# A hybrid decoder layer in split fp32: SBUF pools in a new order, and the first down-projection steps fetched during the last up unit

## The chip, the cores and the metric

One core of a Trainium2 chip. The metric is the device time of one execution in microseconds. The kernel before takes 1019.38 us in the median of 3 runs (1019.26 to 1019.62). In this text 1 KB is 1024 bytes, and an address is an offset within one of SBUF's 128 partitions.

## The reference

One decoder layer over x of 1024 positions by 1024 channels, all in float32, with two sublayers, each followed by a residual and a layer norm:

```python
h = x @ w_in + b_in                                   # 1024 -> 2048
u, v = split(gelu(h[:, :1024]))                       # 4 heads of 128
y_a = u * (causal(w_spatial) @ layernorm(v) + b_spatial)   # in chunks of 128 positions
y_b = silu(layernorm(conv31(a * sigmoid(g))))         # causal depthwise conv, 31 taps; a, g = the rest of h
x1 = layernorm(2**0.25 * x + concat(y_a, y_b) @ w_out + b_out)
h2 = conv3(x1 @ w_up)                                 # 1024 -> 2*2816, causal depthwise conv, 3 taps
out = layernorm(2**0.25 * x1 + (silu(h2[:, :2816]) * h2[:, 2816:]) @ w_down)
```

## The kernel before

**Numbers.** Each operand of a matmul is split into two fp32r tiles: hi, a ScalarE copy (`split`, line 73), and lo, the rest (line 76, on VectorE or GpSimd). A product is three matmuls: hi·hi, hi·lo, lo·hi. A matmul here has weights of 128x128 and a moving operand of 128x512.

**Input projection** (`mm_steps`, L213). 16 tiles of w_in, two of them interleaved at first, each over 8 tiles of x by 2 halves by 3. The weights are `w..h` and `w..l`, the moving operands `xhi` and `xlo`. VectorE computes the 31-tap convolution meanwhile (L261).

**Output projection** (`out_steps`, L535). For each of 8 position tiles s, over 8 tiles k of w_out. The weights are `yah`, `yal`, `ybh`, `ybl`, the moving operands `woh` and `wol`; tile 0 of w_out lies in pool `w`. Then the layer norm, the transposes (`x1_T`, `x1_T2`) and sums (`x1_sums`) that make x1's operands for the up projection.

**Up units.** Unit 0 is plain (L771). Units 1 to 21 each make one gate tile and one value tile (PSUM `upg`, `upv`) by a Strassen-like scheme of 7 products instead of 8 (`prod`, L623), each of 4 k by 3 = 12 matmuls. The moving operands are b11, b21, b22 (pool `a`) and t1 to t4 (pool `f`), the weights are split per unit by `prep_unit`. `unit` keeps partial results in raw tiles `pa`, `pb` (last read at L720 and L719). `gate_tile` and `value_tile` do the 3-tap convolution (L632 on ScalarE, L635 on VectorE), the gate and the product (L649), and store the result to DRAM as `hd[f]` (L651). Odd units use the PSUM pool `un`, even ones `mm`.

**Down projection.** 2 halves th of the positions by 22 steps f. `down_prep(th, f)` (L809) loads w_down[f] (`dr`, SP's queue) and splits it into `dh` and `dl` (pool `a`), loads `hr` from `hd[f]` and splits it into `ho` (hi and lo). `down_mm` (L822) has `ho` as the weights and `dh`, `dl` as the moving operand; for each step 4 position tiles s by 2 halves by 3 = 24 matmuls. Steps are prepared two ahead. Tiles s = 0 and 1 of a half accumulate in the PSUM pool `dn`, which takes the place of `un`; s = 2 and 3 in `mm`. The last 4 steps of the second half are done tile by tile, with the final layer norm (`finish`) behind each.

**Order.** The program is written in the order of the steps, and a list scheduler at compile time arranges the instructions of all engines from it by priority (written order) and by a model of when things are ready. Each engine then runs its list in order. A tile waits until the earlier tile in its buffer has been read; a pool opened after others were closed takes their addresses and waits for them.

**Pools** (lines 48 to 54, and where they are opened), with their addresses in the program as built; the first 16 KB are a DMA scratch area:

| pool | holds | KB |
|---|---|---|
| const | columns, identity, ones | 16.1 to 19.0 |
| w | 3 raw tiles, 2 `whi`, 2 `wlo` of 4 KB | 19.0 to 47.0 |
| a | 16 tiles of 4 KB (tag A) | 47.0 to 111.0 |
| xr | 8 tiles of 4.1 KB | 111.0 to 144.0 |
| r | 3 tiles of 4 KB | 144.0 to 156.0 |
| st | small rows | 156.0 to 158.3 |
| b, then f, then g | 16 tiles of x and w_out; then 16 tiles t1 to t4; then 4 `hr` of 2 KB and 6 `ho` of 4 KB | 158.4 to 222.4 (g to 190.4) |

Of the kernel before, what the change touches and what calls it, by code (L numbers as in the profile page):

```python
# [43 lines left out]
def build(tc, xT, x, w_in, w_out, w_up, w_down, cvec, wsT, rows, bsp, out):  # L44
# [3 lines left out]
    with tc.tile_pool(name="const", bufs=1) as cp, tc.tile_pool(name="w", bufs=1) as wp, tc.tile_pool(  # L48
        name="a", bufs=16
    ) as ap_, tc.tile_pool(name="xr", bufs=8) as xp, tc.tile_pool(name="r", bufs=3) as rp, tc.tile_pool(  # L50
# [13 lines left out]
        def load(src, name, pool=None, tag="raw", eng=None):  # L64
# [60 lines left out]
        with tc.tile_pool(name="b", bufs=16) as bp, tc.tile_pool(name="ps", bufs=2, space=PSUM) as psp:  # L125
# [7 lines left out]
            warm = wp.tile([P, 1024], F32, tag="raw", name="warm", bufs=3)  # L133
# [7 lines left out]
            def raw_w(i):  # L141
                w_raw[i] = wp.tile([P, 1024], F32, tag="raw", name=f"wr{i}", bufs=3)
# [423 lines left out]
            def x1_T(s):  # L566
                so = s % 4
                if so == 0:
                    xb[0, 0], xb[1, 0] = xop("b11"), xop("b21")
                    braw.extend(wp.tile([P, 2, 512], F32, tag="raw", name=f"braw{i}", bufs=3) for i in range(2))  # L570
# [43 lines left out]
        with tc.tile_pool(name="f", bufs=1) as fp:  # L614
            ups, uw = {}, {}

            def unit_ps(f, pool, tag):
                ups[f] = [pool.tile([P, 1024], F32, tag=tag, name=f"up{q}{f}", bufs=2) for q in "gv"]

            def prod(out, w, x, first, last):  # L620
                for k in range(4):
                    for i, (a, b) in enumerate(((0, 0), (0, 1), (1, 0))):
                        nc.tensor.matmul(  # L623
                            out, w[a][:, ts(k, P)], x[b][k // 2][:, k % 2],
                            start=first and k == 0 and i == 0, stop=last and k == 3 and i == 2,
                            skip_group_check=True,
                        )

            def conv3(ct, ps, c, halves=((0, 1024),)):
                w = lambda k: col(C_CFW + 3 * ct + k)  # L630
                for a, b in halves:
                    nc.scalar.activation(c[:, a:b], ps[:, a:b], AF.Identity, bias=col(C_CFB + ct), scale=w(2))  # L632
                    for k, sh in ((1, 1), (0, 2)):
                        o = max(a, sh)
                        nc.vector.scalar_tensor_tensor(  # L635
                            out=c[:, o:b], in0=ps[:, o - sh : b - sh], scalar=w(k), in1=c[:, o:b], op0=ALU.mult,
                            op1=ALU.add,
                        )

            def gate_tile(f, halves=((0, 1024),)):  # L640
                cg = rp.tile([P, 1024], F32, tag="R", name=f"cg{f}")
                conv3(f, ups[f][0], cg, halves)
                nc.scalar.activation(cg, cg, AF.Silu)
                return cg

            def value_tile(f, cg, halves=((0, 1024),)):
                cval = rp.tile([P, 1024], F32, tag="R", name=f"cv{f}")
                conv3(NF + f, ups[f][1], cval, halves)
                nc.vector.tensor_tensor(out=cg, in0=cg, in1=cval, op=ALU.mult)  # L649
                hd[f] = dp.tile([P, S], F32, name=f"hd{f}")  # L650
                nc.sync.dma_start(hd[f], cg)  # L651

            raws = {}

            def xt(name):
                return xp.tile([P, PAD + S], F32, tag="x", name=name)[:, 0:1024]

            def load_unit(f):
                if f < NF:
                    raws[f] = []  # L660
                    for i in range(2):
                        t = xt(f"ur{f}_{i}")
                        nc.sync.dma_start(t, w_up[f + i * NF])
                        raws[f].append(t)

            def op_tile(name, n):
                if n % 2:
                    t = wp.tile([P, 1024], F32R, tag=("whi", "wlo")[n // 2 % 2], name=name, bufs=2)
                else:
                    t = A(F32R, name)  # L670
                return t[:, 0:512], t[:, 512:1024]

            nop = [0]

            def split_op(raw, name):
                hi, lo = op_tile(name, nop[0])
                nop[0] += 1
                split(raw, hi, lo, nc.scalar, nc.gpsimd)
                return hi, lo

            def prep_unit(f):
                if f >= NF:
                    return
                (g, v), tt = raws[f], nc.vector.tensor_tensor
                a11, a12, a21, a22 = g[:, 0:512], g[:, 512:1024], v[:, 0:512], v[:, 512:1024]
                sa, sb = xt(f"sa{f}"), xt(f"sb{f}")
                s1, s2, s3, s4 = sa[:, 0:512], sa[:, 512:1024], sb[:, 0:512], sb[:, 512:1024]
                w = uw[f] = {}
                w[1] = split_op(a11, f"wa{f}")
                w[2] = split_op(a12, f"wb{f}")  # L690
                tt(out=s1, in0=a21, in1=a22, op=ALU.add)
                tt(out=s2, in0=s1, in1=a11, op=ALU.subtract)  # L692
                w[6] = split_op(s2, f"ws2{f}")
                w[5] = split_op(s1, f"ws1{f}")
                tt(out=s3, in0=a11, in1=a21, op=ALU.subtract)  # L695
                w[7] = split_op(s3, f"ws3{f}")
                tt(out=s4, in0=a12, in1=s2, op=ALU.subtract)
                w[3] = split_op(s4, f"ws4{f}")
                w[4] = split_op(a22, f"wd{f}")

            def unit(f):
                z, y = ups[f][0][:, 0:512], ups[f][0][:, 512:1024]
                x, w22 = ups[f][1][:, 0:512], ups[f][1][:, 512:1024]
                w = uw[f]
                sa = wp.tile([P, 1024], F32, tag="raw", name=f"pa{f}", bufs=3)
                sb = wp.tile([P, 1024], F32, tag="raw", name=f"pb{f}", bufs=3)
                p1, u2, p5 = sa[:, 0:512], sa[:, 512:1024], sb[:, 0:512]
                v = nc.vector.tensor_tensor
                prod(x, w[1], xb[0, 0], True, False)
                prod(z, w[2], xb[1, 0], True, True)  # L710
                nc.scalar.copy(p1, x)  # L711
                prod(x, w[6], xt_[2], False, False)
                v(out=z, in0=z, in1=p1, op=ALU.add)
                prod(y, w[5], xt_[1], True, False)
                nc.scalar.copy(u2, x)
                prod(x, w[7], xt_[3], False, False)
                nc.scalar.copy(p5, y)
                prod(y, w[3], xb[1, 1], False, True)
                v(out=w22, in0=x, in1=p5, op=ALU.add)  # L719
                v(out=y, in0=y, in1=u2, op=ALU.add)  # L720
                prod(x, w[4], xt_[4], False, True)


            xt_ = {}
            with tc.tile_pool(name="tx", bufs=2, space=PSUM) as txp:
                xb[0, 1], xb[1, 1] = xop("b12"), xop("b22")
                for i in range(1, 5):
                    xt_[i] = xop(f"t{i}", fp)

                def x1_T2(s):  # L730
                    so, t = s % 4, xs_[s]
                    sl = ts(so, P)
                    tps = []
                    for g in range(2):
                        tp = txp.tile([P, 4, P], F32, tag=f"tx{g}", name=f"x1u{s}_{g}")
                        for c in range(4):
                            nc.tensor.transpose(tp[:, c], t[:, ts(g * 4 + c, P)], ident)
                        for i in range(2):
                            split(
# [47 lines left out]
                for q in range(2):  # L787
                    first_steps(q, 1, range(KT))
# [191 lines left out]
```

## Time and profile before

| | |
|---|---|
| median of 3 runs | 1019.38 us |
| the profiled execution | 1018.94 us |
| its span, first to last instruction | 1017.1 us |
| mean granted TensorE clock | 0.988 |
| instructions | 11752, of them 4344 matmuls |

In the rows further down, PE is TensorE, PEld its weight load, DVE VectorE, ACT ScalarE, POOL GpSimd, SP SyncE, and SPq SP's DMA queue. L822 is line 822 of the kernel. `pd<-dh,ho` means that tile pd is written from dh and ho. Times are in us from the start of the span unless they are marked ns; `x12` counts instructions. An arrow in brackets says how long the engine idled before and what ended it.

### The profile page before, as it was taken

What the parts mean: (1) busy time and instruction counts of PE and PEld (TensorE: products, weight loads), DVE (VectorE), ACT (ScalarE), POOL (GpSimd) and SP (SyncE); (2) the same over time, 40 slices, a digit from 0 to 9 for tenths busy, and PEclk for the clock granted to TensorE, in tenths of its full rate; (3) what the DMA queues carried; (4) which work ended last, traced back from release to release, by engine and by line L of the source; (5) the groups of instructions that cost most, each with busy time, mean ns of one, the idle gap of its engine ahead of it and who ended that gap; (6) DMA issues with size and microseconds to landing.
All of it is one profiled execution on the core that took longest, in us unless ns stands there. A gap on an engine that the chain in (4) does not pass through costs nothing.

```text
span 1017.1 us, 11752 instructions
## 1 busy us (share of the span) xinstructions
PE 988.5 (97%) x4344; PEld 798.4 (78%) x4344; DVE 677.2 (67%) x890; ACT 443.5 (44%) x661; POOL 532.5 (52%) x341
## 2 busy tenths in 40 slices
PE   8999999999997899999999999999979999999996
PEld 5888888878886678888888888888868888888885
DVE  4798999986489975665665675675454444672417
ACT  5233764854624644444443453453444323343302
POOL 4145944684916974454454454544436544488402
PEclk9999999999998899999999999999989999999999
DMA  8111121311520231132122123123458534336202
GB/s 318 60 42 43 42 104 42 125 63 42 187 83 21 84 125 63 63 105 81 63 87 100 63 83 104 63 75 111 153 184 294 175 126 154 132 129 234 98 0 83
DMA packets 33177, 106.84 MB, mean 105 GB/s; under 512 B 3680, under 2 KB 4064, under 8 KB 33120
## 3 DMA queue, kind: packets, MB, share of 16 engines
q1 hardware_dynamic: 33120, 106.09, 30.0%
q8 instruction: 34, 0.56, 0.2%
q14 instruction: 23, 0.19, 0.1%
HBM read 86.16 MB, written 19.92 MB: 104 GB/s over the span
## 4 chain that ended last, share of the span: by engine, by line
PE 87%; DVE 8%; DMA 2%; ACT 1%; issue 1%; SPq 0%; DVEq 0%; ACTq 0%
PE pd L822 24%; PE upv L623 21%; PE ps L213 16%; PE upg L623 16%; PE po L535 8%; DMA xraw<-in_xT 1%; DVE tq L757 1%; DVE wol L76 1%; DVE tq L756 1%; DVE sa L692 1%; PE sv L374 1%; DVE cg L635 1%; DMA hr<-hd 0%; DVE sb L695 0%; ACT woh L73 0%
## 5 line engine op out<-in xcount | busy, mean ns | idle before, releaser
L822 PE MATMUL pd<-dh,ho 128*128 128x512 f32 x688 | 216.4, 395 | 5.7 <-ACT ho L73 5.7
L822 PEld LDWEIGHTS pd<-dh,ho 128*128 128x128 f32 x688 | 129.8, 189 | 38.5 <-ACT ho L73 6.1
L76 POOL TENSOR_TENSOR dl<-dr,dh 128x1024 fp32r<-128x1024 f32 x44 | 108.6, 2476 | 97.7 <-ACT dh L73 97.7
L76 DVE TENSOR_TENSOR ho<-hr,ho 128x512 fp32r<-128x512 f32 x44 | 87.0, 1988 | 105.9 <-ACT ho L73 105.9
L822 PE MATMUL pd<-dl,ho 128*128 128x512 f32 x344 | 138.1, 401 | 0.0
L261 DVE SCALAR_TENSOR_TENSOR acc<-ybin,cv,acc 128x512 f32<-128x512 f32 x196 | 134.3, 747 | 0.9 <-ACT acc L255 0.3
L76 POOL TENSOR_TENSOR ws<-sb,ws 128x512 fp32r<-128x512 f32 x42 | 55.5, 1322 | 83.7 <-ACT ws L73 83.7
L73 ACT CAST dh<-dr 128x1024 fp32r<-128x1024 f32 x44 | 46.1, 1048 | 121.1 <-issue 80.7
L822 PEld LDWEIGHTS pd<-dl,ho 128*128 128x128 f32 x344 | 65.2, 189 | 14.9
L719 DVE TENSOR_TENSOR upv<-upv,pb 128x512 f32<-128x512 f32 x21 | 14.7, 699 | 86.2 <-PE upv L623 86.2
L76 POOL TENSOR_TENSOR ws<-sa,ws 128x512 fp32r<-128x512 f32 x42 | 58.7, 1400 | 7.8 <-ACT ws L73 7.5
L635 DVE SCALAR_TENSOR_TENSOR cg<-upg,cv,cg 128x1023 f32<-128x1023 f32 (+4 forms) x46 | 56.6, 1231 | 8.2 <-ACT cg L632 7.5
L76 POOL TENSOR_TENSOR wa<-ur,wa 128x512 fp32r<-128x512 f32 x21 | 27.5, 1311 | 63.9 <-ACT wa L73 61.5
L623 PE MATMUL upv<-t2h,ws 128*128 128x512 f32 x168 | 57.5, 404 | 1.9 <-ACT pa L711 1.9
L623 PE MATMUL upg<-b21h,wb 128*128 128x512 f32 x168 | 58.2, 391 | 0.5 <-POOL wb L76 0.5
L73 ACT CAST ws<-sb 128x512 fp32r<-128x512 f32 x42 | 26.1, 622 | 74.6 <-PE upv L623 72.2
L635 DVE SCALAR_TENSOR_TENSOR cv<-upv,cv,cv 128x1023 f32<-128x1023 f32 (+4 forms) x46 | 56.6, 1231 | 1.0 <-ACT cv L632 0.4
L623 PE MATMUL upg<-t1h,ws 128*128 128x512 f32 x168 | 56.5, 397 | 0.0
L623 PE MATMUL upv<-t4h,wd 128*128 128x512 f32 x168 | 56.4, 396 | 0.0
L623 PE MATMUL upv<-t3h,ws 128*128 128x512 f32 x168 | 56.3, 396 | 0.0
L623 PE MATMUL upv<-b11h,wa 128*128 128x512 f32 x168 | 55.5, 392 | 0.5 <-DVE cg L635 0.3
L623 PE MATMUL upg<-b22h,ws 128*128 128x512 f32 x168 | 55.3, 390 | 0.0
(411 smaller groups left out, 2354.3 us busy)
## 6 DMA issues: line engine op xcount, KB each, us to landing
ur<-in_w_up SPq DMA_DIRECT2D x44, 512.0 KB, 3.5
dr<-in_w_down SPq DMA_DIRECT2D x44, 512.0 KB, 4.0
hd<-cg SPq DMA_DIRECT2D x22, 512.0 KB, 2.9
hr<-hd SPq DMA_DIRECT2D x44, 256.0 KB, 3.2
wr<-in_w_in SPq DMA_DIRECT2D x14, 512.0 KB, 3.2
xres<-in_x SPq DMA_DIRECT2D x8, 512.0 KB, 3.5
wor<-in_w_out SPq DMA_DIRECT2D x8, 512.0 KB, 3.2
x1d<-xres SPq DMA_DIRECT2D x8, 512.0 KB, 2.6
```

The costliest lines, as they stand in the source:

```text
L73: nc.scalar.copy(hi, raw)
L76: lo_eng.tensor_tensor(out=lo, in0=raw, in1=hi.bitcast(F32), op=ALU.subtract)
L213: nc.tensor.matmul(ps[hf] if isinstance(ps, list) else ps[:, ts(hf, 512)], wt[:, ts(k, P)], xt(k, hf), start=first and k == 0, stop=(not f ...
L261: nc.vector.scalar_tensor_tensor(out=xs(0) if k == 0 else acc, in0=xs(k), scalar=w(k), in1=first if n == 0 else acc, op0=ALU.mult, op1=ALU ...
L374: nc.tensor.matmul(sv[:, c], a[:, g * 4 + c], whl[:, b, h], start=i == 0, stop=i == 2)
L535: nc.tensor.matmul(po[:, ts(hf, 512)], a, b[:, ts(hf, 512)], start=first and i == 0, stop=last and i == 2)
L623: nc.tensor.matmul(out, w[a][:, ts(k, P)], x[b][k // 2][:, k % 2], start=first and k == 0 and i == 0, stop=last and k == 3 and i == 2, ski ...
L635: nc.vector.scalar_tensor_tensor(out=c[:, o:b], in0=ps[:, o - sh : b - sh], scalar=w(k), in1=c[:, o:b], op0=ALU.mult, op1=ALU.add,)
L692: tt(out=s2, in0=s1, in1=a11, op=ALU.subtract)
L719: v(out=w22, in0=x, in1=p5, op=ALU.add)
L756: tt(out=t3[:, q], in0=t2[:, q], in1=raw, op=ALU.subtract)
L822: nc.tensor.matmul(pd, hh[f][a][:, ts(s % 4, P)], wd[f][b][:, c0:c1], start=first and i == 0, stop=last and i == 2,)
```

## The change

The line numbers are those of the kernel before; a piece that was only moved to another indentation is left out.

1. Pools `w`, `a`, `b` now stand one after the other behind `const`. Pool `b` stays open to the end: it holds x and w_out, then t1 to t4 (before in `f`), then `ho` (before in `g`), all in tag B with 16 buffers. Raw tiles have a pool of their own, `raw`, with 3 buffers of 4 KB and 3 for `hr` (before 4). Pools `f` and `g` are gone.
2. The scratch area is 1,024 bytes instead of 16,384.
3. `down_prep` for steps 0, 1 and 2 is written in the last up unit, behind its matmuls and ahead of its convolution; before, steps 0 and 1 came behind that unit, and step 2 with step 0's matmuls.
4. The matmuls of down steps 0 and 1 are written first for s = 2, then 3, then 0, then 1; before, s = 0 to 3 in each step. From step 2 on, everything is as before.

```diff
     with tc.tile_pool(name="const", bufs=1) as cp, tc.tile_pool(name="w", bufs=1) as wp, tc.tile_pool(
         name="a", bufs=16
-    ) as ap_, tc.tile_pool(name="xr", bufs=8) as xp, tc.tile_pool(name="r", bufs=3) as rp, tc.tile_pool(
+    ) as ap_, tc.tile_pool(name="b", bufs=16) as bp, tc.tile_pool(name="raw", bufs=3) as rawp, tc.tile_pool(
+        name="xr", bufs=8
+    ) as xp, tc.tile_pool(name="r", bufs=3) as rp, tc.tile_pool(
         name="st", bufs=3
...
-            t = (pool or wp).tile([P, 1024], F32, tag=tag, name=name, **({"bufs": 3} if tag == "raw" else {}))
+            t = rawp.tile([P, 1024], F32, tag="raw", name=name)
...
-                [pool.tile([P, 2, 512], F32R, tag="xo", name=f"{name}{q}{i}", bufs=16) for i in range(2)] for q in "hl"
+                [pool.tile([P, 2, 512], F32R, tag="B", name=f"{name}{q}{i}") for i in range(2)] for q in "hl"
...
-        with tc.tile_pool(name="b", bufs=16) as bp, tc.tile_pool(name="ps", bufs=2, space=PSUM) as psp:
+        with tc.tile_pool(name="ps", bufs=2, space=PSUM) as psp:
...
-                    xt_[i] = xop(f"t{i}", fp)
+                xt_[i] = xop(f"t{i}", bp)
...
+        def down_prep(th, f):
+            raw = load(w_down[f], f"dr{th}_{f}")
+            hi, lo = (A(F32R, f"d{q}{th}_{f}") for q in "hl")
+            split(raw, hi, lo, nc.scalar, nc.gpsimd)
+            wd[f] = (hi, lo)
+            hr = rawp.tile([P, 512], F32, tag="hr", name=f"hr{th}_{f}")
+            nc.sync.dma_start(hr, hd[f][:, ts(th, 512)])
+            h = bp.tile([P, 2, 512], F32R, tag="B", name=f"ho{th}_{f}")
+            split(hr, h[:, 0], h[:, 1], nc.scalar, nc.vector)
+            hh[f] = (h[:, 0], h[:, 1])
...
+                prep_unit(f + 1)
+                if f == NF - 1:
+                    for n in range(3):
+                        down_prep(0, n)
+                value_tile(f, gate_tile(f))
...
-            steps = [(th, f) for th in range(2) for f in range(NF)]
-            for n in range(2):
-                down_prep(*steps[n])
-            for n, (th, f) in enumerate(steps):
-                if n + 2 < len(steps):
-                    down_prep(*steps[n + 2])
+            def ahead(n):
+                if n < 2 * NF:
+                    down_prep(n // NF, n % NF)
...
+            for s in (2, 3):
+                open_(s)
+                for f in range(2):
+                    down_step(s, f)
+            for s in (0, 1):
+                open_(s)
+                for f in range(2):
+                    down_step(s, f)
+            ahead(3)
+            for n in range(2, 2 * NF):
+                th, f = n // NF, n % NF
+                ahead(n + 2)
...
-    nc = bacc.Bacc("TRN2", target_bir_lowering=False, num_devices=1)
+    nc = bacc.Bacc("TRN2", target_bir_lowering=False, num_devices=1, dynamic_dma_scratch_size=1024)
```

## Rows read from the trace of the kernel before

**Rows 1.** The page, part 1: busy us (share of the span) xinstructions.

```profile
PE 988.5 (97%) x4344; PEld 798.4 (78%) x4344; DVE 677.2 (67%) x890; ACT 443.5 (44%) x661; POOL 532.5 (52%) x341
```

**Rows 2.** Windows: stretch, us, busy us (count) of each engine, granted clock, DMA.

```profile
38.00:117.00 79.00, 79.00 (x339) 63.57 (x338) 75.17 (x110) 30.91 (x40) 39.56 (x26) 1.00 0.12 42
117.00:190.00 73.00, 73.00 (x360) 60.45 (x359) 71.37 (x165) 47.23 (x76) 37.94 (x24) 1.00 0.20 70
310.00:373.00 63.00, 54.47 (x220) 42.09 (x218) 62.79 (x90) 33.76 (x72) 54.10 (x49) 0.89 0.20 67
399.00:754.00 355.00, 355.00 (x1536) 288.57 (x1534) 214.12 (x210) 157.54 (x232) 165.88 (x123) 1.00 0.26 89
764.00:1000.00 236.00, 236.00 (x1013) 189.95 (x1012) 109.28 (x95) 71.88 (x92) 122.19 (x49) 1.00 0.41 143
```

**Rows 3.** Waits of TensorE: who waited for whom, us in total, times, longest.

```profile
PE pd L822 <- ACT ho L73: 5.7, 1, 5.7
```

**Rows 4.** The chain of waits, 745 to 760 us: start, us, what.

```profile
745.82 2.81 PE upv L623 x12
748.63 2.74 PE upg L623 x12
...
754.20 4.98 DMA hr<-hd
...
759.21 0.63 ACT ho L73
```

**Rows 5.** Timeline of TensorE, last up unit to first down matmuls: start, us, instruction.

```profile
745.89 0.40 PE L623 MATMUL upv<-t3l,ws 128*128 128x512 f32 x1
...
746.60 0.40 PE L623 MATMUL upv<-t3l,ws 128*128 128x512 f32 x1
...
749.39 0.39 PE L623 MATMUL upg<-b22l,ws 128*128 128x512 f32 x1
...
750.07 0.39 PE L623 MATMUL upg<-b22l,ws 128*128 128x512 f32 x1
...
753.78 0.40 PE L623 MATMUL upv<-t4h,wd 128*128 128x512 f32 x1
759.88 0.80 PE L822 MATMUL pd<-dh,ho 128*128 128x512 f32 x1 [5.71 <-ACT ho L73]
...
763.30 0.62 PE L822 MATMUL pd<-dh,ho 128*128 128x512 f32 x2
```

**Rows 6.** The chain of waits: unbroken stretches of matmuls in three stages.

```profile
37.95 79.88 PE ps L213 x341
...
275.55 11.20 PE po L535 x48
...
759.88 242.53 PE pd L822 x1032
```

**Rows 7.** Timelines of SP's queue, ScalarE, GpSimd and VectorE, 734 to 760 us.

```profile
734.97 0.33 SPq L66 DMA_DIRECT2D dr<-in_w_down  x1
...
749.47 3.48 SPq L66 DMA_DIRECT2D dr<-in_w_down  x3
...
752.87 1.05 ACT L73 CAST dh<-dr 128x1024 fp32r<-128x1024 f32 x1 [5.48 <-DMA dr<-in_w_down]
...
754.00 2.35 POOL L76 TENSOR_TENSOR dl<-dr,dh 128x1024 fp32r<-128x1024 f32 x1 [4.08 <-ACT dh L73]
...
748.74 0.70 DVE L719 TENSOR_TENSOR upv<-upv,pb 128x512 f32<-128x512 f32 x1 [3.57 <-PE upv L623]
751.41 0.70 DVE L720 TENSOR_TENSOR upg<-upg,pa 128x512 f32<-128x512 f32 x1 [1.97 <-PE upg L623]
...
758.64 1.27 DVE L635 SCALAR_TENSOR_TENSOR cv<-upv,cv,cv 128x1022 f32<-128x1022 f32 x1
```

**Rows 8.** Tile ho (ns min/median/max, starts) and, by form, a like VectorE group.

```profile
L76 DVE TENSOR_TENSOR ho<-hr,ho x44: 635/2473/2905, 759.9 to 975.1; 128x512 fp32r<-128x512 f32 x44
...
L76 DVE TENSOR_TENSOR xlo<-xraw,xhi 128x512 fp32r<-128x512 f32 x2 | 1.4, 693 | 3.6 <-ACT xhi L73 3.6
```

More of the change, by code (lines that the diff above doesn't have):

```diff
@@ L62, in A, with load @@
             return ap_.tile(list(shape), dt, tag="A", name=name)
-        def load(src, name, pool=None, tag="raw", eng=None):
-            t = (pool or wp).tile([P, 1024], F32, tag=tag, name=name, **({"bufs": 3} if tag == "raw" else {}))
+        def load(src, name):
+            t = rawp.tile([P, 1024], F32, tag="raw", name=name)
             nc.sync.dma_start(t, src)
@@ L569, in x1_T @@
                     xb[0, 0], xb[1, 0] = xop("b11"), xop("b21")
-                    braw.extend(wp.tile([P, 2, 512], F32, tag="raw", name=f"braw{i}", bufs=3) for i in range(2))
+                    braw.extend(rawp.tile([P, 2, 512], F32, tag="raw", name=f"braw{i}") for i in range(2))
                 t = xs_[s]
@@ L613, in build, with unit_ps @@
         hd = {}
[L614 to L622, printed above, removed]
+        ups, uw = {}, {}
+        def unit_ps(f, pool, tag):
+            ups[f] = [pool.tile([P, 1024], F32, tag=tag, name=f"up{q}{f}", bufs=2) for q in "gv"]
@@ new lines, in prod, with conv3 @@
+        def prod(out, w, x, first, last):
+            for k in range(4):
+                for i, (a, b) in enumerate(((0, 0), (0, 1), (1, 0))):
+                    nc.tensor.matmul(
+                        out, w[a][:, ts(k, P)], x[b][k // 2][:, k % 2],
+                        start=first and k == 0 and i == 0, stop=last and k == 3 and i == 2,
+                        skip_group_check=True,
+                    )
+        def conv3(ct, ps, c, halves=((0, 1024),)):
+            w = lambda k: col(C_CFW + 3 * ct + k)
+            for a, b in halves:
+                nc.scalar.activation(c[:, a:b], ps[:, a:b], AF.Identity, bias=col(C_CFB + ct), scale=w(2))
+                for k, sh in ((1, 1), (0, 2)):
+                    o = max(a, sh)
+                    nc.vector.scalar_tensor_tensor(
+                        out=c[:, o:b], in0=ps[:, o - sh : b - sh], scalar=w(k), in1=c[:, o:b], op0=ALU.mult,
+                        op1=ALU.add,
+                    )
@@ new lines, in build, with xt, load_unit, op_tile @@
+        raws = {}
+        def xt(name):
+            return xp.tile([P, PAD + S], F32, tag="x", name=name)[:, 0:1024]
+        def load_unit(f):
+            if f < NF:
+                raws[f] = []
+                for i in range(2):
+                    t = xt(f"ur{f}_{i}")
+                    nc.sync.dma_start(t, w_up[f + i * NF])
+                    raws[f].append(t)
+        def op_tile(name, n):
+            if n % 2:
+                t = wp.tile([P, 1024], F32R, tag=("whi", "wlo")[n // 2 % 2], name=name, bufs=2)
+            else:
+                t = A(F32R, name)
+            return t[:, 0:512], t[:, 512:1024]
@@ new lines, in build, with split_op, prep_unit @@
+        nop = [0]
+        def split_op(raw, name):
+            hi, lo = op_tile(name, nop[0])
+            nop[0] += 1
+            split(raw, hi, lo, nc.scalar, nc.gpsimd)
+            return hi, lo
+        def prep_unit(f):
+            if f >= NF:
+                return
+            (g, v), tt = raws[f], nc.vector.tensor_tensor
+            a11, a12, a21, a22 = g[:, 0:512], g[:, 512:1024], v[:, 0:512], v[:, 512:1024]
+            sa, sb = xt(f"sa{f}"), xt(f"sb{f}")
+            s1, s2, s3, s4 = sa[:, 0:512], sa[:, 512:1024], sb[:, 0:512], sb[:, 512:1024]
+            w = uw[f] = {}
+            w[1] = split_op(a11, f"wa{f}")
+            w[2] = split_op(a12, f"wb{f}")
+            tt(out=s1, in0=a21, in1=a22, op=ALU.add)
+            tt(out=s2, in0=s1, in1=a11, op=ALU.subtract)
+            w[6] = split_op(s2, f"ws2{f}")
+            w[5] = split_op(s1, f"ws1{f}")
+            tt(out=s3, in0=a11, in1=a21, op=ALU.subtract)
+            w[7] = split_op(s3, f"ws3{f}")
+            tt(out=s4, in0=a12, in1=s2, op=ALU.subtract)
+            w[3] = split_op(s4, f"ws4{f}")
+            w[4] = split_op(a22, f"wd{f}")
@@ new lines, in unit @@
+        def unit(f):
+            z, y = ups[f][0][:, 0:512], ups[f][0][:, 512:1024]
+            x, w22 = ups[f][1][:, 0:512], ups[f][1][:, 512:1024]
+            w = uw[f]
+            sa = rawp.tile([P, 1024], F32, tag="raw", name=f"pa{f}")
+            sb = rawp.tile([P, 1024], F32, tag="raw", name=f"pb{f}")
+            p1, u2, p5 = sa[:, 0:512], sa[:, 512:1024], sb[:, 0:512]
+            v = nc.vector.tensor_tensor
+            prod(x, w[1], xb[0, 0], True, False)
+            prod(z, w[2], xb[1, 0], True, True)
+            nc.scalar.copy(p1, x)
+            prod(x, w[6], xt_[2], False, False)
+            v(out=z, in0=z, in1=p1, op=ALU.add)
+            prod(y, w[5], xt_[1], True, False)
+            nc.scalar.copy(u2, x)
+            prod(x, w[7], xt_[3], False, False)
+            nc.scalar.copy(p5, y)
+            prod(y, w[3], xb[1, 1], False, True)
+            v(out=w22, in0=x, in1=p5, op=ALU.add)
+            v(out=y, in0=y, in1=u2, op=ALU.add)
+            prod(x, w[4], xt_[4], False, True)
@@ new lines, in build, with x1_T2, x1_sums, first_steps @@
+        xt_ = {}
+        with tc.tile_pool(name="tx", bufs=2, space=PSUM) as txp:
+            xb[0, 1], xb[1, 1] = xop("b12"), xop("b22")
+            for i in range(1, 5):
+                xt_[i] = xop(f"t{i}", bp)
+            def x1_T2(s):
+                so, t = s % 4, xs_[s]
+                sl = ts(so, P)
+                tps = []
+                for g in range(2):
+                    tp = txp.tile([P, 4, P], F32, tag=f"tx{g}", name=f"x1u{s}_{g}")
+                    for c in range(4):
+                        nc.tensor.transpose(tp[:, c], t[:, ts(g * 4 + c, P)], ident)
+                    for i in range(2):
+                        split(
+                            tp[:, 2 * i : 2 * i + 2], xb[g, 1][0][i][:, :, sl], xb[g, 1][1][i][:, :, sl],
+                            nc.scalar, nc.vector,
+                        )
+                    tps.append(tp)
+                return tps
+            def x1_sums(s, tps):
+                sl = ts(s % 4, P)
+                ta, tb = (xt(f"tq{s}_{i}").rearrange("p (a c d) -> p a c d", a=2, c=4) for i in range(2))
+                t1, t2, t3, t4 = ta[:, 0], ta[:, 1], tb[:, 0], tb[:, 1]
+                tt = nc.vector.tensor_tensor
+                for i in range(2):
+                    q = slice(2 * i, 2 * i + 2)
+                    raw = braw[i][:, :, sl]
+                    tt(out=t1[:, q], in0=tps[0][:, q], in1=raw, op=ALU.subtract)
+                    tt(out=t2[:, q], in0=tps[1][:, q], in1=t1[:, q], op=ALU.subtract)
+                    tt(out=t3[:, q], in0=t2[:, q], in1=raw, op=ALU.subtract)
+                    tt(out=t4[:, q], in0=xb[1, 0][0][i][:, :, sl].bitcast(F32), in1=t2[:, q], op=ALU.subtract)
+                    tt(out=t4[:, q], in0=t4[:, q], in1=xb[1, 0][1][i][:, :, sl].bitcast(F32), op=ALU.add)
+                for n, t in ((2, t2), (1, t1), (3, t3), (4, t4)):
+                    for i in range(2):
+                        split(
+                            t[:, 2 * i : 2 * i + 2], xt_[n][0][i][:, :, sl], xt_[n][1][i][:, :, sl],
+                            nc.scalar, nc.gpsimd,
+                        )
+            unit_ps(0, mmp, "mm")
+            def first_steps(q, hf, ks):
+                for k in ks:
+                    for n, (a, b) in enumerate(((0, 0), (0, 1), (1, 0))):
@@ L653, in build @@
[L653 to L671, printed above, removed]
@@ L701, in unit @@
[L701 to L721, printed above, removed]
@@ L793, in build @@
-            with tc.tile_pool(name="un", bufs=2, space=PSUM) as unp:
-                for f in range(1, NF):
-                    unit_ps(f, *((unp, "un") if f % 2 else (mmp, "mm")))
-                    load_unit(f + 1)
-                    unit(f)
-                    prep_unit(f + 1)
-                    value_tile(f, gate_tile(f))
-        with tc.tile_pool(name="g", bufs=1) as gp, tc.tile_pool(name="dn", bufs=2, space=PSUM) as dnp:
+                            ups[0][q][:, ts(hf, 512)], up0[q][a][:, ts(k, P)], xb[k // 4, hf][b][k % 4 // 2][:, k % 2],
@@ new lines, in first_steps @@
+                            start=k == 0 and n == 0, stop=k == KT - 1 and n == 2,
+                        )
+            load_unit(1)
+            tps = {}
+            for q in range(2):
+                for k in range(KT):
+                    first_steps(q, 0, [k])
+                    if q == 0 and k in (0, 2, 4):
+                        tps[4 + k // 2] = x1_T2(4 + k // 2)
+                        x1_sums(4 + k // 2, tps[4 + k // 2])
+                    if q == 1 and k == 5:
+                        tps[7] = x1_T2(7)
+                        x1_sums(7, tps[7])
@@ new lines, in build @@
+            for q in range(2):
+                first_steps(q, 1, range(KT))
+            prep_unit(1)
+            hv = ((0, 512), (512, 1024))
+            value_tile(0, gate_tile(0, hv), hv)
+        wd, hh = {}, {}
+        def down_prep(th, f):
+            raw = load(w_down[f], f"dr{th}_{f}")
+            hi, lo = (A(F32R, f"d{q}{th}_{f}") for q in "hl")
+            split(raw, hi, lo, nc.scalar, nc.gpsimd)
+            wd[f] = (hi, lo)
[4 more added lines that the diff above has]
+            hh[f] = (h[:, 0], h[:, 1])
@@ L803, in build @@
+        with tc.tile_pool(name="un", bufs=2, space=PSUM) as unp:
+            for f in range(1, NF):
+                unit_ps(f, *((unp, "un") if f % 2 else (mmp, "mm")))
+                load_unit(f + 1)
+                unit(f)
+                prep_unit(f + 1)
[3 more added lines that the diff above has]
+                value_tile(f, gate_tile(f))
+        with tc.tile_pool(name="dn", bufs=2, space=PSUM) as dnp:
             g2 = rp.tile([P, 1024], F32, tag="R", name="g2row")
@@ L914, in build @@
                 for s in range(4 * th, 4 * th + 4):
[L915 to L916 removed]
+                    down_step(s, f)
                     if th == 0 and f == NF - 1:
```

146 lines of the change are left out of this document (20 added, 126 removed).

## The prediction

> **What bounds the kernel now.** The page's busy times come first: TensorE is busy for 97% of the span [rows 1]. The stages then show where another engine sets the pace [rows 2]: from 38 to 190 us VectorE is busy for 146.5 of 152 us beside a full TensorE; from 310 to 373 us VectorE has 62.8 of 63 us and TensorE only 54.5 at a granted clock of 0.89; in the up units (399 to 754 us) and the down projection (764 to 1000 us) TensorE is full and nothing else is near it. So there are two ways to save: take away TensorE's waits, and shorten the distance from one matmul to the next. TensorE's longest wait is one of 5.7 us, where the down projection begins, for ScalarE's copy of the first `ho` [rows 3].
>
> **Distance between matmuls.** I read it from the chain and from starts in the timeline. In one and the same unit the 12 matmuls of t3 take 2.81 us and the 12 of b22 take 2.74 [rows 4]; inside the products t3l follows t3l, three matmuls on, after 0.70 to 0.71 us (234 ns each) and b22l follows b22l after 0.68 us (227 ns each) [rows 5]. Weights, engine and PSUM traffic are of the same kind. What differs is where the moving operand lies: b22 in pool `a` (47 to 111 KB of a partition), t3 in pool `f` (158 to 222 KB). The other stages fit: the input projection moves x from pool `b` (158 KB up), 79.88 us for 341 matmuls, 234.3 ns; the output projection moves w_out from `b`, 11.20/48 = 233.3 ns; in the down projection the moving operand is in `a`, but the weights `ho` are in `g` (158 KB up), 242.53 us for 1032 [rows 6], 233.5 ns without the 1.55 us of slow start worked out below. I conclude that a matmul with one operand high costs 234, and one with both low 227.
>
> By the Trainium skill, "TensorE: Matmul & The Clock Gate", section Back-to-back issue gap, an isolated full-clock matmul of 512 columns follows the last after N/2.4 + 2.5, some 216 ns, with no term for an address, and "SBUF — State Buffer", section Who interferes with whom, has it that TensorE never waits on anyone at its ports. By those pages the new layout is worth nothing; the rows above disagree, both in the level and in the difference between two products of one unit. That case is the second rival.
>
> **The change, part by part. Pools.** Worked out from the pool lines, `w` then lies at 4 to 20 KB, `a` at 20 to 84, `b` (x, w_out, t1 to t4, `ho`) at 84 to 148, 16 tiles of 4 KB; raw tiles, `xr`, `r` and `st` above that. No row has a matmul of these shapes with an operand between 111 KB and 158 KB. The bounds: if everything above the last low row (111 KB) is slow, 6 of the 16 tiles of `b` gain; if all below the first high row is fast, all 16 do. A worse price than 234 is not excluded by a row, but both sides of the gap show only 227 and 234. By the nearest row (the middle is 134.7 KB) 12 of 16 gain, 0.75, and this I take. In full it would be worth:
> - t1 to t4 in 21 units: 21 x 48 = 1008 matmuls x 7.5 ns = 7.6 us, TensorE-bound, all of it counts: 5.7 at 0.75.
> - b11, b21, b22: 21 x 36 = 756 matmuls at 228.3 instead of 226.7, since a few at the seams with t go at the slow distance: at most 1.2, I take 0.6.
> - Down: 1032 x 6.8 ns = 7.0 us, TensorE-bound: 5.3 at 0.75.
> - Output projection: 7 of 8 w_out tiles, 336 x 6.6 = 2.2 us: 1.6. VectorE has room ahead of it.
> - Input projection: 16 x 48 = 768 x 7.6 = 5.8 us: 4.4. Here VectorE's convolution taps fill 146.5 of 152 us, so TensorE can run ahead only by what VectorE can make up, 5.5 us at best and nothing at worst: I take half, 2.2.
> Sum 15.4 us; bounds 7.7 (6 tiles) and 20.5 (16 tiles).
>
> **The first down steps.** Now: the last up matmul starts at 753.78 and is done with its columns at 754.01; the first down matmul starts at 759.88 [rows 5], 5.87 us later. The chain says why: `hr` of step 0 is issued at 754.20, lands after 4.98 us, and its ScalarE copy comes at 759.21 [rows 4], because `g` lies on the addresses of `f` and opens only when the last unit is done. Then the first 8 matmuls take from 759.88 to 763.30, 3.42 us where 8 x 233.5 = 1.87 is usual: 1.55 us lost at half the granted clock. Together 7.4 us.
>
> After: each of three steps issues two loads on SP's queue, two ScalarE copies (1.05 us for `dh`, 0.63 for `ho`), one GpSimd subtraction (2.35) and one VectorE subtraction (0.64 to 2.9, median 2.5) [rows 4, 7, 8]. `hr` has its own place and `ho` takes the buffers of t2 and t1, whose last products end by 745.8 [rows 4]. Step 0 can be whole by then: its `dr` is loaded at 734.97 already in the kernel before. Step 1 cannot come sooner than its raw buffer, which unit 21's `pb` gives up at 749.4: `dr` at 749.47, ScalarE's copy at 752.87, GpSimd's from 754.00 to 756.35 [rows 7], all as before; its `hr` is queued on SP behind that `dr` and lands about 753. So from 754.0 TensorE has s = 2 and 3 of step 0 (12 matmuls, 2.8 us, to 756.8), then step 1 of both (to 759.6). These write the `mm` banks, free since unit 20. s = 0 and 1 need the banks of unit 21, which VectorE has emptied at 758.64 + 1.27 = 759.9 in the kernel before [rows 7]; now one or two `ho` subtractions of 2.5 us may stand ahead of it in VectorE's queue, and TensorE, which issues in order, would wait with all that follows. From both sides: 0.3 us of waiting without them, 5.3 with two. I take 2.0, since VectorE is idle after 752.1 and may do one there; the clock is then taken as kept: gain 7.4 - 2.0 = 5.4. Queued behind on SP, the store of hd21 can be late without cost: it is read in step 21. GpSimd, idle for 4 us ahead of 754.00, has only these steps to do. Three `hr` buffers instead of four, and `ho` 16 instead of 6, cost nothing, since loads run two steps (11 us) ahead; that fails only if a load took longer than a step's 5.6 us twice over. The smaller scratch costs nothing: every DMA here is issued by SP.
>
> **Sum.** 15.4 + 5.4 = 20.8 us less. The profiled execution took 1018.94 us, 0.44 below the median 1019.38: 998.1, and 998.6 for a median.
>
> **Rivals.**
> - *The wait moves to the PSUM banks.* If ScalarE and VectorE take all three steps ahead of unit 21's convolution, step 2's `dr` included (raw buffer free at 752.1, 4 us to land), the banks are empty some 4 us later, at 764; TensorE idles from 759.6 and the clock may fall again: of 5.4 us about 1.5 is left, time 1002.5. For it: the three steps are written ahead of that convolution. Against: engines are given ready work first. Chance 0.10; its pool part varies as in the forecast.
> - *The distance is not a matter of place.* If 234 goes with what the tiles are and not with their address, only the 5.4 us of the handover come: 1013.9. The pages above amount to this. Against it are products of one unit and three stages that all sort by address. 0.13.
> - *Slower: VectorE at high addresses.* `xr` moves from 111-144 to 166-199 KB and `r` to 199-211 KB, and VectorE sets the pace for 209 busy us (38 to 190 and 310 to 373). If its operations took 12% longer there, that adds 25 us: 1023. It decides from 10% up. Against: `ho` at 158 to 190 KB shows a shortest subtraction of 635 ns, while `xlo` from `a` has a mean of 693 for the same shape [rows 8]. 0.04.
>
> **How the numbers follow.** Forecast, with a step somewhere between 111 and 158 KB: 0.70, from 1018.94 - 7.7 - 5.4 = 1005.8 to 1018.94 - 20.5 - 5.4 = 993.0, plus 0.44, likeliest 998.6. With the handover's 2 us either way and the first rival this gives 992 to 1010; the second and third rivals stay outside. What this kernel's timing can tell from no change is 0.2%, 2 us. Faster: 0.70 + 0.10 + 0.13 = 0.93; slower 0.05, the third rival and a mishap of order; the same 0.02.
>
> **What would show it.** Right: t and `ho` matmuls 227 ns apart for most tiles and 234 for the topmost, with one address where it changes; VectorE's operations as long as before; a first down matmul within 1 us of the last up matmul, then a wait for VectorE L635 of 0.3 to 4 us; less gain from 38 to 190 us than 4.4. Wrong: t products still at 2.81 us, or a longer stretch 310 to 373 us.

## The result and the profile after

The changed kernel takes 996.49 us in the median of 4 runs (996.12 to 998.15), the kernel before 1019.50 beside it: a ratio of 0.9776, 95% interval 0.9759 to 0.9793. The profiled execution took 996.77 us (span 994.7), 22.2 us less than that of before.

The page, part 1, of the changed kernel (busy us, share of the span, instructions), against [rows 1]:

```profile
PE 964.9 (97%) x4344; PEld 796.5 (80%) x4344; DVE 664.7 (67%) x890; ACT 444.8 (45%) x661; POOL 534.9 (54%) x341
```

As many matmuls, 23.6 us less of busy TensorE. The chain of waits of the changed kernel (start, us, what) says where:

```profile
270.96 10.90 PE po L537 x48
...
708.68 2.72 PE upv L624 x12
711.40 2.72 PE upg L624 x12
...
719.11 2.72 PE upg L624 x12
...
737.50 6.13 DMA dr<-in_w_down
743.63 0.02 issue
743.65 1.05 ACT dh L75
744.71 0.07 issue
744.77 2.39 POOL dl L78
747.16 0.04 issue
747.21 232.66 PE pd L828 x1018
```

The output projection's 48 matmuls take 10.90 us instead of 11.20 [rows 6], 227 ns each. The products of t2 (708.68) and t1 (711.40) take 2.72 us, and so does that of b22 (719.11): the 2.81 us of t products [rows 4] are gone. Over the whole trace the mean distance of each kind (without the waits) is 226.6 to 228.0 ns (x, w_out, b11, b21, b22, t1 to t4, `dh`, `dl`), with no slower tile at the top of pool `b`, at 148 KB. VectorE's tap of the convolution runs as before, 747 ns a piece at the old place and 744 at the new one (first the row of before, then that of the changed kernel: busy us, mean ns):

```profile
L261 DVE SCALAR_TENSOR_TENSOR acc<-ybin,cv,acc 128x512 f32<-128x512 f32 x196 | 134.3, 747 | 0.9 <-ACT acc L255 0.3
L263 DVE SCALAR_TENSOR_TENSOR acc<-ybin,cv,acc 128x512 f32<-128x512 f32 x196 | 134.2, 744 | 0.9 <-ACT acc L257 0.3
```

The windows of the changed kernel (stretch, us, busy us (count) of each engine, granted clock, DMA share, GB/s; the second is the stretch 310 to 373 us of before, shifted) answer to [rows 2]:

```profile
38.00:117.00 79.00, 79.00 (x354) 65.50 (x353) 77.35 (x115) 32.29 (x41) 42.05 (x28) 1.00 0.13 46
...
299.00:362.00 63.00, 51.45 (x229) 40.29 (x227) 61.64 (x91) 32.30 (x74) 50.42 (x47) 0.95 0.20 72
...
373.00:732.00 359.00, 359.00 (x1585) 297.32 (x1585) 221.26 (x221) 167.00 (x245) 173.47 (x129) 1.00 0.26 89
```

From 38 to 117 us TensorE issues 354 matmuls where it issued 339: VectorE, at 77.35 of 79 us, kept up better than I feared. From 299 to 362 VectorE still sets the pace.

At the handover, TensorE's timeline (start, us, instruction, idle time and who ended it):

```profile
740.93 0.39 PE L624 MATMUL upv<-t4h,wd 128*128 128x512 f32 x1
741.16 0.62 PE L828 MATMUL pd<-dh,ho 128*128 128x512 f32 x2
...
744.75 0.73 PE L828 MATMUL pd<-dh,ho 128*128 128x512 f32 x2 [0.71 <-ACT dh L75]
747.21 0.50 PE L828 MATMUL pd<-dl,ho 128*128 128x512 f32 x1 [1.72 <-POOL dl L78]
...
748.82 0.63 PE L828 MATMUL pd<-dl,ho 128*128 128x512 f32 x1
749.25 1.05 PE L828 MATMUL pd<-dh,ho 128*128 128x512 f32 x2
```

The first down matmul now starts 0.23 us behind the last up matmul: the 5.7 us for ScalarE's `ho` [rows 3] are gone. But 12 matmuls later TensorE waits for step 1, first `dh`, then `dl`, and the matmuls behind that come 427 ns apart, as 748.82 and 749.25 show: half the granted clock, which a window from 748.4 to 751.8 gives as 0.55, against 1.00 ahead of the waits and from 752 on. The chain names the cause: `dr` of step 1 is issued at 737.50, when VectorE has read `pb` (its L720 starts at 736.78), takes 6.13 us to land, and ScalarE and GpSimd follow.

The gain by stage, from the starts of the matmuls at the seams counted from the first matmul, in us. The loss at the handover counts, from the last up matmul over the first 200 down matmuls, the distances that stand out (over 245 ns, waits included), each with what it has above 227 ns: 7.48 before, 4.59 after.

| stage | forecast | measured |
|---|---|---|
| input projection | 2.2 | 4.95, of which 1.34 go at the next stage's start, on ScalarE's `u`: 3.6 |
| output projection | 1.6 | 1.7 |
| units 0 and 1 (VectorE's) | 0 | 0.1 |
| units 2 to 21 | 6.3 | 7.4 |
| handover | 5.4 | 7.48 - 4.59 = 2.9 |
| down projection | 5.3 | 6.9 |
| sum | 20.8 | 22.6 |

### The profile page after: what moved, and what is told of

Same layout as the page of the kernel before. It is cut to its first block, busy times and chain, and to the rows that moved or that the text cites. A ratio compares the mean times of both kernels' runs of the same rounds, so it can differ in the third digit from the quotient of the medians.

```text
span 994.7 us, 11745 instructions
## 1 busy us (share of the span) xinstructions
PE 964.9 (97%) x4344; PEld 796.5 (80%) x4344; DVE 664.7 (67%) x890; ACT 444.8 (45%) x661; POOL 534.9 (54%) x341
## 4 chain that ended last, share of the span: by engine, by line
PE 76%; DVE 17%; ACT 3%; DMA 2%; issue 1%; SPq 0%; POOL 0%; DVEq 0%; ACTq 0%
PE pd L828 23%; PE upv L624 20%; PE upg L624 15%; PE ps L215 8%; PE po L537 8%; DVE acc L263 6%; DMA xraw<-in_xT 1%; DVE cg L636 1%; DVE tq L758 1%; DVE tq L757 1%; DMA dr<-in_w_down 1%; DVE wol L78 1%; DVE ast L351 1%; DVE sa L693 1%; ACT vt L363 1%
## 5 line engine op out<-in xcount | busy, mean ns | idle before, releaser
L828 PE MATMUL pd<-dh,ho 128*128 128x512 f32 x688 | 213.4, 391 | 0.7 <-ACT dh L75 0.7
L828 PE MATMUL pd<-dl,ho 128*128 128x512 f32 x344 | 134.7, 392 | 1.7 <-POOL dl L78 1.7
L78 DVE TENSOR_TENSOR ho<-hr,ho 128x512 fp32r<-128x512 f32 x44 | 77.8, 1790 | 61.2 <-ACT ho L75 61.2
L720 DVE TENSOR_TENSOR upv<-upv,pb 128x512 f32<-128x512 f32 x21 | 14.7, 698 | 78.9 <-PE upv L624 78.9
L624 PE MATMUL upv<-t2h,ws 128*128 128x512 f32 x168 | 55.3, 390 | 1.9 <-ACT pa L712 1.9
```

The costliest lines, as they stand in the source:

```text
L78: lo_eng.tensor_tensor(out=lo, in0=raw, in1=hi.bitcast(F32), op=ALU.subtract)
L624: nc.tensor.matmul(out, w[a][:, ts(k, P)], x[b][k // 2][:, k % 2], start=first and k == 0 and i == 0, stop=last and k == 3 and i == 2, ski ...
L828: nc.tensor.matmul(pd, hh[f][a][:, ts(s % 4, P)], wd[f][b][:, c0:c1], start=first and i == 0, stop=last and i == 2,)
```

## The experiments

**What makes 234 ns?** In the program before, pools `w` and `a` start 96 bytes past a multiple of 128 (19,424 and 48,096), but `b`, `f` and `g` on one (162,176). In the changed kernel all three start 96 past one. Each slice that a matmul reads starts a multiple of 512 bytes into its tile, and a tile of these pools has 4096 bytes, so all operands of one pool share one remainder. So my rows, which sorted by address, sort just as well by whether the moving operand and the weights start at the same remainder. The first pair of runs parts the two readings: one mends the remainder and leaves `b` high, one spoils it and leaves `b` low.

```diff
 # b_shift96: the kernel before; 96 unused bytes, cleared once, in front of b, f and g
-    ) as stp, tc.tile_pool(name="mm", bufs=2, space=PSUM) as mmp, tc.tile_pool(
+    ) as stp, tc.tile_pool(name="pad", bufs=1) as padp, tc.tile_pool(name="mm", bufs=2, space=PSUM) as mmp, tc.tile_pool(
+        pad = padp.tile([P, 24], F32, name="pad")
+        nc.vector.memset(pad, 0.0)
 # a_shift32: the changed kernel; 32 unused bytes between a and b
-    ) as ap_, tc.tile_pool(name="b", bufs=16) as bp,
+    ) as ap_, tc.tile_pool(name="pad", bufs=1) as padp, tc.tile_pool(name="b", bufs=16) as bp,
+        pad = padp.tile([P, 8], F32, name="pad")
+        nc.vector.memset(pad, 0.0)
```

> The kernel before, with 96 unused bytes ahead of pools b, f and g, so that they begin at 158.47 KB instead of 158.38: still above every other pool, but 96 bytes past a multiple of 128, as w and a do; before, they began on a multiple of 128. Place theory (operands above some address between 148 and 158 KB are slow): t products stay at 234 ns per matmul, down at 233, time 1019.5. Alignment theory (slow where the two operands of a matmul start at different offsets in a line of 64 or 128 bytes): all at 227 ns, and the time falls by the matmul part of the change, some 17 to 20 us, to 1000 to 1002; the wait of 5.7 us ahead of the down projection stays in both.

Measured: 1001.16 us (998.85 to 1005.49), ratio 0.9812, interval 0.9768 to 0.9856. Rows of its chain, then of its waits (engine, what, releaser: us, times, longest):

```profile
271.79 10.90 PE po L537 x48
...
747.85 236.49 PE pd L824 x1032
```

```profile
PE pd L824 <- ACT ho L75: 5.8, 1, 5.8
```

> The changed kernel, with 32 unused bytes between pools a and b: b stays low (84.0 to 148.0 KB) but begins on a multiple of 128, while a and w stay 96 bytes past one. Place theory: nothing changes, 227 ns, 996.5 us. Alignment theory: x, w_out, t and ho operands go to 231 to 238 ns, mean 234, and the time to 1014 to 1017.

Measured: 1014.20 us, in a single run. Its chain:

```profile
275.04 11.18 PE po L539 x48
...
721.69 2.79 PE upv L626 x12
724.48 2.80 PE upg L626 x12
...
760.03 237.81 PE pd L830 x1018
```

So place is out. With `b` still above 158 KB, 96 bytes bring 10.90 us for 48 matmuls and 236.49 us for the 1032 of [rows 6], while the wait at the handover stays: 18.6 us less than the 1019.74 of the kernel before beside it (by the interval, 15 to 24), from 96 unused bytes. With `b` low, 32 bytes take nearly all of it away: 11.18 us, t products at 2.79 and 2.80, and 237.81 us for the same 1018 matmuls that take 232.66 in the changed kernel. The pad of `a_shift32` moves the raw tiles, `xr`, `r` and `st` as well, but that of `b_shift96` moves `b`, `f` and `g` alone, so the tiles of the other engines are not the cause.

**Is height or the remainder itself of any account?** `a_b_high` has the changed kernel's pool `b` on top, at 149.5 to 213.5 KB with the remainder kept (the pool line moved behind `st`, 96 unused bytes ahead of it). `a_all_0` adds 32 unused bytes to `const`, so that `w`, `a` and `b` all start on a multiple of 4096.

> The changed kernel with pool b opened above raw, xr, r and st: it lies at 149.5 to 213.5 KB, 96 bytes past a multiple of 128 like w and a. Place theory: t, x, w_out and ho operands at 234 ns but for the lowest two or three tiles of b, time 1013 to 1017. Alignment theory: all at 227 ns, 996.5 us.

> The changed kernel with 32 unused bytes in const, so that w, a and b all begin on a multiple of 128 instead of 96 bytes past one. Place theory: no change, 227 ns, 996.5 us. Alignment theory by difference of the two operands: no change either. If what counts is each operand's own offset (a start on a multiple of 128 being the slow one): all matmuls at 234 ns or more, 1018 us or more; if it is the fast one, below 227 ns and below 996 us.

Measured: 998.35 us in a single run of `a_b_high`, and 996.51 for `a_all_0` (995.99 to 1000.31; ratio 0.9769, 0.9736 to 0.9801). (The 1000.31 is the profiled execution, which lost some 4 us ahead of the output projection; TensorE waited 1.9 us for ScalarE's `vt` there, and its granted clock was 0.50 from 165.4 to 168.8 us.) In both, 48 output matmuls take 10.90 us and each kind of matmul is at 226 to 228 ns. Neither height nor the remainder alone matters, only whether the two operands agree.

**Agree to how many bytes?** The pad of `a_shift32` at 64, 96, 128 and 256 bytes (`[P, 16]`, `[P, 24]`, `[P, 32]`, `[P, 64]`).

> The changed kernel with 64 unused bytes between pools a and b, so that b starts 32 bytes past a multiple of 128 and w and a 96 past one: they differ by 64 bytes within 128, and are equal within 64. If operands must agree within a line of 64 bytes: 227 ns throughout and 996.5 us. If within 128: x, w_out, t and ho operands at 234 ns, 1013 to 1016 us.

> The changed kernel with 96 unused bytes between pools a and b, so that b starts 64 bytes past a multiple of 128: 32 bytes off w and a within a line of 64, in the other 64 bytes of a line of 128 than in the run with 32. Slow by both rules: x, w_out, t and ho operands at 233 to 234 ns, 1013 to 1016 us. 227 ns here would mean that neither a line of 64 nor one of 128 bytes is what counts.

> The changed kernel with 128 unused bytes between the pools a and b: the moving operands of pool b start 96 bytes past a multiple of 128 as before, but their distance to the weights is no longer a multiple of 256 or 512. Theory (the starts of the two operands must agree modulo 128): all classes of matmuls stay at about 227 ns, time 995 to 999 us. Rival (they must agree modulo 256 or 512; in all quick layouts so far the distance happened to be a multiple of 512): t, x, w_out and down matmuls at 230 to 234 ns, time 1011 to 1016 us.

> The changed kernel with 256 unused bytes between the pools a and b. Theory (modulo 128): 227 ns, 995 to 999 us. Rival (modulo 512): 230 to 234 ns, 1011 to 1016 us. Rival (modulo 256): slow with 128 bytes, 227 ns and 995 to 999 us here.

Measured, in a single run each: 1015.17, 1015.30, 1011.66 and 996.65 us. The order of work is the same in these four and in `a_shift32`: every engine has the same list of instructions, so nothing but the pad and the addresses differs. Of the chains of the four, in this order, the rows of the output projection and of the down projection:

```profile
277.12 11.03 PE po L539 x48
...
760.97 237.81 PE pd L830 x1018
```

```profile
274.82 11.20 PE po L539 x48
...
760.18 238.77 PE pd L830 x1018
```

```profile
275.02 11.17 PE po L539 x48
...
758.40 236.85 PE pd L830 x1018
```

```profile
270.23 10.90 PE po L539 x48
...
747.46 232.66 PE pd L830 x1018
```

128 bytes apart is slow, 256 is as quick as none. So the theory that I had up to then, "modulo 128", falls too, and its rival holds: the starts must agree modulo 256. (In the quick layouts ahead of these the distance happened to be a multiple of 512, which is why they could not tell.) Of the differences tried, 32, 64, 96 and 128 are slow, and so is the 160 of the kernel before; less than 32, and 192 and 224, were not tried. They are not all equally slow: at 64, w_out comes at 229.8 ns (11.03 / 48) and x at 229, but the down matmuls at 233.3. Why these differ is open. A product whose operands agree is slow at first when it follows one whose operands do not: in `a_shift32`, where b22 comes behind t3, its first seven distances are 225 to 240 ns in the mean of the units, the last five 226.7. Open, too, is what collides: a matmul's moving operand with its own weights, or with the next matmul's, which are loaded while it runs. All the weights of a stretch have one remainder here, so no run parts these two.

**What holds the first down steps up?** `a_raw5` gives every raw tile five buffers instead of three (`bufs=5` at each tile with tag "raw"), so that step 1's load has a buffer early. `a_fetch_behind` writes the three `down_prep` behind unit 21's `value_tile` instead of ahead of it.

> The changed kernel with 5 raw buffers of 4 KB instead of 3 (also for the loads of the input projection). Theory of the handover: the waits of 0.7 and 1.7 us of the first down matmuls and the half clock after them come from step 1's load of w_down, which gets its raw buffer only when unit 21 has read pb; with two more buffers step 1 is loaded and split ahead of time, the loss of 4.6 us goes down to 0 to 1.5 and the time by 3 to 4.5 us, to 992 to 993.5. Rival: the matmuls of s = 0 and 1 then wait for unit 21's PSUM banks instead, as long as before: 995.5 to 997.

Measured: 1004.25 us (1003.71 to 1008.46), ratio 0.9853, interval 0.9831 to 0.9876: 8 us slower than the changed kernel. TensorE's waits:

```profile
PE sv L376 <- DVE bst L317: 4.8, 1, 4.8
PE upv L624 <- ACT pa L712: 4.5, 1, 4.5
...
PE pd L828 <- DVE cv L636: 1.6, 1, 1.6
```

At the handover it did what the theory said: the waits for `dh` and `dl` went, the loss fell from 4.59 to 2.16 us, and what is left is the wait for unit 21's PSUM banks (VectorE's `cv`), the prediction's first rival in small. But the scheduler used the buffers everywhere: loads and splits came earlier, the order changed in earlier stages, the first row is new, and the second was 1.9 us in the changed kernel. The time forecast, 992 to 993.5, was missed for that. The run settles what held step 1 up and shows nothing for a better kernel.

> The changed kernel with the three early down steps written behind the last unit's convolution instead of ahead of it; they keep their own buffers. Theory: what held the first matmul up was that hr and ho had to wait for the place of the last unit's operands, so a place of their own gives most of it wherever they are written: within 1.5 us of 996.5. Rival: the place in the written order is what counts; the first down matmul then waits again for ScalarE's copy of ho, 4 to 6 us, and the time is 999 to 1001.

Measured: 997.22 us (995.47 to 997.83), ratio 0.9769, interval 0.9750 to 0.9787. The scheduler makes the same list for each engine from either order of writing, instruction for instruction; so this is the changed kernel once more. Where the call is written is not what brings the steps forward. That it is the buffers of their own, which `hr` and `ho` find free, follows from the chain of before [rows 4], where `hr` is issued only when the last unit is done; no run varies them alone, nor point 4 of the change, the order of s.

**A better version.** `a_own_dr` gives the loads of steps 0 and 1 alone two buffers of their own, and orders these two loads behind unit 21's load on SP's queue, so that the lists of TensorE, VectorE, ScalarE and GpSimd stay as they are up to unit 20 or 21. `a_again` is the changed kernel beside it.

```diff
         def down_prep(th, f):
-            raw = load(w_down[f], f"dr{th}_{f}")
+            if th == 0 and f < 2:
+                raw = rawp.tile([P, 1024], F32, tag="dr", bufs=2, name=f"dr{th}_{f}")
+                with tc.issue_after(lastload[0]):
+                    nc.sync.dma_start(raw, w_down[f])
+            else:
+                raw = load(w_down[f], f"dr{th}_{f}")
```

> The changed kernel with two staging buffers of their own for the rows of w_down of the down steps 0 and 1, their loads ordered on SP's queue behind the last up unit's loads, so that the order of work up to the middle of unit 21 stays. Theory (what is left of the handover, 4.6 us, is step 1's load waiting for a raw buffer that the last unit holds, and the half clock behind it): the waits 0.7 <-ACT dh and 1.7 <-POOL dl at the first down matmuls go, loss at the handover falls to 0 to 2.2 us, time lower than the changed kernel's by 2 to 4 us (992.5 to 995). Rival (PSUM banks, released by VectorE's last cv, end the wait anyway at nearly the same time): a wait <-DVE cv of 1 to 2 us takes their place and the time falls by less than 1.5 us (995 to 997).

> The changed kernel itself, unaltered, beside the one with own buffers on the same chip: 996.0 to 997.5 us, the waits at the first down matmuls 0.7 <-ACT dh and 1.7 <-POOL dl as before.

Measured: 993.20 us (991.88 to 996.36), ratio 0.9741, interval 0.9718 to 0.9763, against 996.44 (996.26 to 996.70), ratio 0.9769, 0.9752 to 0.9786. In the middle it is 3.2 us better, inside the 2 to 4 expected; the two intervals still overlap a little, so the gain is likely and not certain. Its timeline at the handover:

```profile
733.92 0.39 PE L835 MATMUL pd<-dh,ho 128*128 128x512 f32 x1
...
742.76 0.39 PE L624 MATMUL upv<-t4h,wd 128*128 128x512 f32 x1
...
751.37 0.50 PE L835 MATMUL pd<-dl,ho 128*128 128x512 f32 x1 [0.52 <-POOL dl L78]
```

Down matmuls now start at 733.92, between the last products of unit 21, whose t4 begins at 742.76: with the loads of steps 0 and 1 issued at 678.72 and 679.53, the scheduler put 15 down matmuls ahead of the last up matmul. So the variant changes the order as well as the buffers, and no run parts the two. One wait of 0.52 us is left, the granted clock stays at 1.00 from 734 to 760 us, and the loss at the handover is 0.87 us against 4.24 in `a_again`. The rival, a wait of 1 to 2 us for the banks, did not come. `a_again` showed 2.0 us for `dl` and none for `dh` in its list of waits, not the 1.7 and 0.7 that I had written down.

## Why the prediction was right, and where it was not

The time was 996.49 where I said 998.6, in a range of 992 to 1010, and the sign was right. But the reason given for three quarters of the gain was wrong, and two sizes were off in opposite directions: 15.4 us for the matmul distance became 19.7, 5.4 for the handover became 2.9. That the time came so close is luck in two ways: the two errors cancel in part, and the new pool order mends the remainder, at which it did not aim.

- **"A matmul with one operand high costs 234, and one with both low 227"** is the step that failed. The levels were right and the sorting of the rows too; the cause was the remainder of the two starts modulo 256 (`b_shift96`, `a_shift128`, `a_shift256`). The remainders stood in the same pool lines as the addresses; I compared only the addresses. The pool line mends the remainder because `b` now follows `a`, whose 16 tiles of 4096 bytes keep it. In the kernel before, `xr`, `r` and `st` stood between them, and the sizes of `xr` (8 tiles of 4,216 bytes) and `st` do not.
- **"12 of 16 tiles gain"** fell with it: there is no step between 111 and 158 KB, and all 16 gained. Hence t and `b` products 7.4 us instead of 6.3, down 6.9 instead of 5.3. The upper bound of 20.5 for this part, all 16 tiles, was close to the measured 19.7.
- **Input projection**: 4.95 instead of 2.2. TensorE could run ahead for most of what the shorter distance gave (5.8 in the forecast), beside a VectorE at 77.35 of 79 us; 1.34 of it was lost again at the start of the output projection, where ScalarE's `u` came last (TensorE's wait there: 1.8 us, none of it in the list of before).
- **The handover**: the start of the first down matmul was right (0.23 us, "within 1 us"), and 5.87 us of waiting went. Of what takes its place I had the wrong piece. I let step 1 come in time and priced VectorE's release of the PSUM banks at 2.0; TensorE never waited for it. Step 1 itself was late: I had its `dr` land 3.4 us after issue, as in [rows 7], and it took 6.13 (that row was among the shortest: the 44 loads of `dr` took 3.3 to 8.1 us in the kernel before, 4.0 in the median); TensorE was done with step 0's columns at 743.9 and had `dl` of step 1 at 747.16. And "the clock is then taken as kept" failed: behind waits of 0.71 and 1.72 us, 2.5 us apart, seven matmuls ran at half clock and two partly, 1.6 us of the 4.59. Both are gone in `a_own_dr`, where steps 0 and 1 are loaded early and the order is new.
- **The rivals.** *The wait moves to the PSUM banks*: not in the changed kernel, in part in `a_raw5` (1.6 us). *The distance is not a matter of place*: true in its words, wrong in its price, since the change also mends the remainder; `a_shift32`, at 1014.20, is what it would have looked like (1013.9 forecast, 1014.0 by its own sum). By the Trainium skill, "SBUF — State Buffer", section Who interferes with whom, TensorE reads the moving operand and the weights through two independent ports. The runs show a distance that depends on how the two starts stand to each other, for which that section has no term. The section Operand start alignment of the same page says of itself that it is about legality and not speed; these runs supply a speed. *Slower, VectorE at high addresses*: out, 744 ns against 747.
- **What costs nothing**: three `hr` buffers instead of four and the later store of hd21 left no wait in TensorE's list.

## What to carry to other kernels

When two products with the same shapes run at two distances, compare every property of their operands' starts, the remainders as well as the height, and vary one of them alone before naming a cause; here 96 unused bytes brought some 18.6 of the 23.0 us. For matmuls of this form, lay out pools so that the moving operands and the weights start at the same remainder modulo 256, by making the sizes of the pools between them multiples of 256. And give a tile that must be early buffers of its own, with its load ordered behind a fixed instruction: more buffers for all (`a_raw5`) let a scheduler reorder stages that had nothing to gain.

## What the runs showed of the hardware that was not expected

- Matmuls of 512 moving fp32r columns, each with its own weight load, follow each other after 226 to 228 ns when the moving operand and the weights start at the same remainder modulo 256, and after 229 to 235 ns, in the mean of each kind of operand, when these differ by 32, 64, 96, 128 or 160 bytes. By the Trainium skill, "TensorE: Matmul & The Clock Gate", section Back-to-back issue gap, a sustained stream of such pairs at 512 columns runs at about 131 ns; no run here comes near it.
- The granted clock fell to half (0.55 from 748.4 to 751.8 us) behind waits of only 0.71 and 1.72 us, though TensorE had been full from 373 to 732 us. In `a_again` one listed wait of 2.0 us had the same behind it (0.50 from 747.8 to 751.2 us). But one of 1.6 us in `a_raw5` and one of 2.0 us at the same place in `a_shift64` and in `a_shift128` left it at 1.00. What decides is not shown.
- The load of step 1's `dr`, 512 KB, took 3.4 us in the kernel before and 6.13 us in the changed one. Other transfers stand beside it there: DMA is busy for 0.78 of its engines' time and moves 264 GB/s from 737.5 to 743.6 us, against 0.47 and 154 GB/s from 749.5 to 752.9 us in the kernel before. That these are the cause was not tested.
